# Which engine adds the block sums of the down and gate weights, and when the gate's first chunks are split

## The chip, the cores and the metric

The kernel runs on one core of a Trainium2 chip. The metric is the device time of one execution in microseconds (us); shorter is better. The engines are named as the profile names them: PE (matrix products, with PEld for its weight loads), DVE (vector), ACT (scalar), POOL (GpSimd) and SP (which here only issues DMAs).

## The reference

One layer of a decoder trunk over 512 tokens of width 1024, in fp32, and a final RMSNorm. The part that the change touches is the end of it:

```
h = rmsnorm(x, ffn_norm[i])
x = x + conv_ffn(h, w_up[i], conv_w[i], conv_b[i], w_down[i])
gate = sigmoid(rmsnorm(x, ple_norm[i]) @ w_ple_gate[i])
x = x + gate * (p[i] @ w_ple[i])
return rmsnorm(x, final_norm)
```

`conv_ffn` multiplies by `w_up` (1024 x 5632), runs a causal convolution of width 3, gates one half by the GELU of the other, and multiplies by `w_down` (2816 x 1024). The gate's weights are 1024 x 1024.

## The kernel before, in words

**Each fp32 product is three.** Every operand is cut into a rounded high part and the rest. For weights `parts` (L64 to 72) does it: ACT casts (`whi`, L69), DVE subtracts (`wlo`, L70). `mm3` (L203 to 207) then issues three matmuls, at L205, L206 and L207. A pair of cut tiles holds 1024 columns, and four pairs are in rotation (`WB = 4`); with `spare` the pair comes from the pool of 37 general 4 KB buffers (`blk`) instead.

**Seven products for eight.** The large square products follow a scheme in which a 2 x 2 block product takes seven block products, P1 to P7. Their weights are four blocks a, b, c, d and sums of them: P1 takes a, P2 takes d, P3 takes c, P5 takes t = b + a, P7 takes s = b + c, P6 takes t + c, P4 takes that + d. Each of them is handled in chunks of two 128-row slices (1024 columns); a product of n = 4 slices has two chunks, c0 and c1. `plan_seven` (L93 to 148) makes for each product and chunk a unit of two functions: `load` brings the blocks in, `cut` makes the high and low part. What computes the sums is its argument `adds`:

- "vector": blocks are loaded as they are, and all sums are DVE additions (L138) in `cut`.
- "some": t = b + a and s = b + c are made by the DMA: `get` loads b on SP's queue and adds the second block with an accumulating DMA on POOL's queue (`add_to`, L106). The additions of c for P6 and of d for P4 are DVE's, at L138.
- "all": as "some", but c and d are added to t by accumulating DMAs too, issued when P5 and P6 have been cut.

**The order.** `todo` is the list of units in the order of their use. `prepare` and `take` (L150 to 160) keep four loaded and two cut ahead of PE (four in the tail). All engines, and SP's and POOL's DMA queues, work in the order of the program, so an instruction that waits holds up all behind it. `seven` (L349 to 407) runs the products in a given order. Where P6 ends, its result is copied from PSUM to SBUF by ACT (`u`, L372), since P7 goes on in the same banks; PE's first matmul of P7 waits for that copy.

**The stages around the change.** The up projection is a loop of 22 steps (L689 to 717), two `proj8` of 24 matmuls each. The down projection is done in three parts, (0,4), (4,4) and (8,3), inside that loop after steps 8, 16 and 21, in the order DOWN = P1, P5, P2, P6, P7, P4, P3, all with "all". Parts 1 and 2 have two full chunks, part 3 a full and a half one. Its results are added to x by DVE (`drain_x`, L682). Then the tail: `turn_half` transposes x (PE L724, scaled by ACT, L727), `embed` multiplies by `w_ple` (L652), the loop that fills `XE` makes the seven operands of the gate (L746 to 757), and the gate's product runs in the order LAST = P5, P1, P6, P7, P4, P2, P3 with "some", as the last large product. Four small operations on POOL (L615) make the norms' factors between part 3 and the gate. After it come the sigmoid, the last sums and the output.

Of the kernel before, what the change touches and what calls it, by code (L numbers as in the profile page):

```python
# [20 lines left out]
KF = FF // P  # L21
# [12 lines left out]
INNER = ("P1", "P5", "P6", "P7", "P4", "P2", "P3")  # L34
DOWN = ("P1", "P5", "P2", "P6", "P7", "P4", "P3")
LAST = ("P5", "P1", "P6", "P7", "P4", "P2", "P3")
# [9 lines left out]
def trunk(ctx, tc, xT, xr, pT, wsT, par, bsp, w_u0, w_u1, w_v, w_ga, w_gb, w_p, w_pl,  # L46
# [28 lines left out]
    todo = []  # L75
# [9 lines left out]
    def pairs_of(n):  # L85

        return [(q, min(2, n - q)) for q in range(0, n, 2)]
# [5 lines left out]
    def plan_seven(w, order=INNER, adds="vector", spare=(), q0=0, n=HK):  # L93

        raw = {}

        def block_of(name, ch):  # L100
            q, m = ch
            return w("abdc".index(name), q0 + q, m)

        def fetch(t, name, ch, **kw):
            o = t[:, :ch[1] * T].rearrange("p (q f) -> p q f", q=ch[1])
            (G if kw else nc.sync).dma_start(o, block_of(name, ch), **kw)  # L106

        def add_to(t, name, ch):
            fetch(t, name, ch, accum_op=ALU.add)

        def get(name, ch, *blocks):
            if (name, ch) not in raw:
                t = raw[name, ch] = block("raw", (CW,))
                fetch(t, blocks[0], ch)
                for z in blocks[1:]:
                    add_to(t, z, ch)
            return raw[name, ch]

        def unit(prod, ch):
            inplace = adds == "vector"  # L120
            t = "a" if inplace else "t"
            need = {"P1": [("a", "a")], "P5": [("b", "b")] if inplace else [("t", "b", "a")],
                    "P6": [] if adds == "all" else [("c", "c")], "P7": [] if inplace else [("s", "b", "c")],
                    "P4": [] if adds == "all" else [("d", "d")], "P2": [("d", "d")], "P3": [("c", "c")]}[prod]
            dst = {"P1": "a", "P5": t, "P6": t, "P7": "b" if inplace else "s", "P4": t, "P2": "d", "P3": "c"}[prod]
            extra = {"P5": "b" if inplace else None, "P6": "c", "P7": "c" if inplace else None, "P4": "d"}.get(prod)
            if adds == "all":
                extra = None
            cols = ch[1] * T

            def load():
                for args in need:
                    get(args[0], ch, *args[1:])

            def cut():
                z = raw[dst, ch]
                if extra:
                    V.tensor_tensor(z[:, :cols], z[:, :cols], raw[extra, ch][:, :cols], op=ALU.add)  # L138
                o = parts(z, cols, spare=prod in spare)
                if adds == "all" and prod in ("P5", "P6"):  # L140
                    add_to(z, "c" if prod == "P5" else "d", ch)
                return o

            todo.append((load, cut))

        for prod in order:
            for ch in pairs_of(n):
                unit(prod, ch)

    def prepare(loads=LOADS):  # L150
        while todo and len(loaded) < loads:
# [5 lines left out]
    def take(ahead=AHEAD, loads=LOADS):  # L157
        while (todo or loaded) and len(ready) <= ahead:
            prepare(loads)
        return ready.pop(0)  # L160
# [7 lines left out]
    def blocks(w):  # L168

        return lambda b, q, m: w[b, q:q + m].rearrange("q p f -> p q f")  # L170

    for w in (w_v, w_ga, w_gb):
        plan_seven(blocks(w))

    def plan_map(g2):
        plan(w_pl[g2].rearrange("p g k d -> p (g k d)"))
# [14 lines left out]
    for i in range(KF):  # L191
        plan(w_up[2 * i].rearrange(flat))
        plan(w_up[2 * i + 1].rearrange(flat))

        part = done_at.get(i // 2) if i % 2 == 0 else done_at.get(KF // 2) if i == KF - 1 else None
        blocks_of_down.append(part)
        if part:
            plan_seven(blocks(w_dn), DOWN, "all", q0=part[0], n=part[1])
    for k in range(2):
        plan(w_ple[k])  # L200
    plan_seven(blocks(w_g), LAST, "some", spare=("P3",))

    def mm3(o, w, a, first, last, **kw):  # L203
        (wh, wl), (ah, al) = w, a
# [141 lines left out]
    ops = {"P1": ("a", "A11"), "P5": ("c", "D"), "P6": ("b", "S2"), "P7": ("b", "S3"), "P4": ("b", "A22"),  # L346
           "P2": ("a", "A12"), "P3": ("c", "E")}

    def seven(op, drain, order=INNER, fill=(), tail=False):  # L349

        fill = list(fill)
        n = len(op)
        ahead = AHEAD + 2 if tail else AHEAD
        bank_of = {}
        begun = set()
        u = [[None, None], [None, None]]

        def step(o, c, w, ch, first):  # L360
            for j, c0, m, t in o:
                for i in range(ch[1]):
                    k = ch[0] + i
                    a = op[k][c]
                    a = [a[:, z, j * P:(j + 1) * P] for z in range(2)]
                    mm3(t, a, [z[:, c0:c0 + m] for z in wslice(w, i, T)], first and k == 0, k == n - 1,
                        skip_group_check=True)

        def copies(i):
            for j in range(2):  # L370
                u[i][j] = work("u")
                S.copy(u[i][j], seeded[j])  # L372

        def minus(p, z):
            j, c0, m, t = p
            o = z[j][:, c0:c0 + m]
            V.tensor_tensor(o, t, o, op=ALU.subtract)
            return o

        for prod in order:  # L380
            b, c = ops[prod]
            if b not in bank_of:
                bank_of[b] = [(j, 0, T, seeded[j] if b == "b" else bank()) for j in range(2 if b != "c" or not tail else 1)]
                if b == "c" and tail:
                    bank_of[b] += [(1, 0, H, bank()[:, :H]), (1, H, H, bank()[:, :H])]
            o = bank_of[b]
            first = b != "b" and b not in begun
            begun.add(b)
            if prod == "P3" and tail:
                ws = [take(ahead) for _ in pairs_of(n)]  # L390
                for p in o:
                    for w, ch in zip(ws, pairs_of(n)):
                        step([p], c, w, ch, False)
                    drain(0, p[0], 1, minus(p, u[0]), p[1])
                continue
            for ch in pairs_of(n):
                step(o, c, take(ahead), ch, first)
                if fill:
                    fill.pop(0)()
            if prod == "P1":  # L400
                for j in range(2):
                    S.copy(seeded[j], o[j][3])
            elif prod == "P6":
                copies(0)
            elif prod == "P7":
                copies(1)
                for p in bank_of["c"]:
                    minus(p, u[1])
                for j in range(2):
                    drain(1, j, 1, u[1][j], 0)  # L410
            elif prod == "P4":
                for j in range(2):
                    drain(1, j, 0, seeded[j], 0)
            elif prod == "P2":
                for p in o:
                    drain(0, p[0], 0, p[3], 0)
            elif prod == "P3":
                for p in o:
                    drain(0, p[0], 1, minus(p, u[0]), 0)
        for f in fill:  # L420
            f()
# [17 lines left out]
    def load(k):  # L439
        if k % 2 == 0:  # L440
            x2.append(block("x"))
        x.append(x2[-1][:, k % 2])
        nc.sync.dma_start(x[k], xT[k])
# [3 lines left out]
    for k in range(KD):  # L447
# [3 lines left out]
        c = take(1, 1)  # L451
# [234 lines left out]

    hc = []
    first = None
    for i in range(KF):  # L689
        if i:  # L690
            o1, o2 = proj8(xg), proj8(xg)
        else:

            o1, o2 = bank(), bank()
            c = [take(), take()]
            for k in range(KD):
                for o, w in zip((o1, o2), c):
                    mm3(o, wslice(w, k), act(xg[k]), k == 0, k == KD - 1)
        a = conv(2 * i, o1)
        S.activation(a, a, AF.Gelu)  # L700
        b = conv(2 * i + 1, o2)
        V.tensor_tensor(a, a, b, op=ALU.mult)
        if i % 2 == 0:
            q = i // 2
            if q % 2 == 0 or any(q == q0 for q0, _ in PARTS):
                t11 = block("a11", (2, 2, H), F32R)
                n11 = 0
            cut_into(t11[:, n11], a[:, :H])
            first = a
        else:  # L710
            z = split(a)
            hc.append(dict(A11=t11[:, n11], A12=z[:, :, :H], A22=z[:, :, H:], **combine(first, a)))
            n11 += 1
        part = blocks_of_down[i]
        if part:
            q0, n = part
            seven(hc[q0:q0 + n], drain_x(q0 + n == KF // 2), DOWN)
# [28 lines left out]
    XE = []  # L746
# [41 lines left out]
                    V.tensor_scalar_mul(ot, ot, r)  # L788
                nc.sync.dma_start(out[b, :, g * T:(g + 1) * T], ot)

    seven(XE, drain_g, LAST, tail=True)


_ORDER = ["xT", "xr", "pT", "wsT", "par", "bsp", "w_u0", "w_u1", "w_v", "w_ga", "w_gb", "w_p", "w_pl",
# [72 lines left out]
```

## Time and profile before

| | |
|---|---|
| median of 3 runs | 807.81 us (807.12 to 807.92) |
| the profiled execution | 809.77 us, its span 808.1 us |
| PE busy | 773.3 us, 96% of the span |
| DVE, ACT, POOL busy | 553.9, 389.6, 60.5 us |
| mean granted clock of PE | 0.986 |

Times of the trace count from the start of the span; the profiled execution is 1.67 us longer than its span. "Idle before" is the time in which an engine had nothing to do ahead of an instruction, with the instruction that released it behind the arrow. A row of PE gives the start and the length of a matmul; they overlap, so that their pace is read from start to start.

### The profile page before, as it was taken

To read this page: it belongs to the slowest core of one execution; us is meant where nothing else is said; L and a number is where in the kernel's file an instruction comes from. 1 tells how busy PE (TensorE), PEld (TensorE's weight loads), DVE (VectorE), ACT (ScalarE), POOL (GpSimd) and SP (SyncE) were. 2 spreads that over 40 slices of the span, in tenths; PEclk is the share of its full clock that TensorE was granted. 3 is DMA by queue.
4 is the path that set the end of the run, shared out by engine and by line. 5 is a ranking of instruction groups with operands and counts; after the bars stand their busy time and mean duration, and the time that the engine had idled before them with its cause. 6 is when DMAs were issued, how large, how long until landed. Compare 5 with 4: busy or idle time off the path is not lost.

```text
span 808.1 us, 9316 instructions
## 1 busy us (share of the span) xinstructions
PE 773.3 (96%) x3458; PEld 635.6 (79%) x3458; DVE 553.9 (69%) x783; ACT 389.6 (48%) x566; POOL 60.5 (7%) x95
## 2 busy tenths in 40 slices
PE   9999999999999999999999997999999799999793
PEld 7888888888888887888888875888888588877673
DVE  7796988774666646336766663676774566778896
ACT  6676745562232324225644543345443434467873
POOL 0000100000122000000000021000013010031101
PEclk9999999999999999999999998999999899999997
DMA  9612225152044256006422369631229862391712
GB/s 350 253 53 79 78 79 183 53 191 96 1 156 150 85 173 218 1 1 268 174 53 66 91 133 269 216 93 46 78 79 212 244 168 78 107 194 26 239 22 104
DMA packets 42493, 104.26 MB, mean 129 GB/s; under 512 B 3664, under 2 KB 3792, under 8 KB 42448
## 3 DMA queue, kind: packets, MB, share of 16 engines
q1 hardware_dynamic: 33760, 85.73, 30.3%
q0 software_dynamic: 7104, 13.63, 10.0%
q10 hardware_dynamic: 1584, 4.31, 1.6%
q8 instruction: 27, 0.44, 0.2%
q14 instruction: 18, 0.15, 0.1%
HBM read 100.51 MB, written 3.15 MB: 128 GB/s over the span
## 4 chain that ended last, share of the span: by engine, by line
PE 47%; issue 27%; DMA 11%; DVE 8%; ACT 5%; POOL 1%; POOLq 0%; SPq 0%; ACTq 0%; DVEq 0%
PE mm L205 10%; PE mm L206 10%; PE mm L207 10%; DMA raw<-in_w_dn 9%; PE sd L205 6%; PE sd L206 6%; PE sd L207 6%; DVE wlo L70 2%; ACT whi L69 2%; DMA pt<-in_pT 1%; DVE raw L138 1%; POOL raw L106 1%; PE mm L514 1%; DVE x L773 0%; DVE ple L784 0%
## 5 line engine op out<-in xcount | busy, mean ns | idle before, releaser
L70 DVE TENSOR_TENSOR wlo<-raw,whi 128x1024 fp32r<-128x1024 f32 (+1 forms) x192 | 225.3, 1182 | 184.2 <-ACT whi L69 183.6
L69 ACT CAST whi<-raw 128x1024 fp32r<-128x1024 f32 (+1 forms) x185 | 189.8, 1032 | 232.4 <-PE mm L206 56.2
L206 PE MATMUL mm<-blk,whi 128*128 128x512 f32 x480 | 186.8, 389 | 0.0
L205 PE MATMUL mm<-blk,whi 128*128 128x512 f32 x480 | 186.4, 390 | 0.3 <-ACT blk L240 0.3
L207 PE MATMUL mm<-blk,wlo 128*128 128x512 f32 x480 | 186.6, 389 | 0.0
L205 PEld LDWEIGHTS mm<-blk,whi 128*128 128x128 f32 x480 | 90.0, 188 | 19.6 <-ACT blk L240 0.9
L206 PEld LDWEIGHTS mm<-blk,whi 128*128 128x128 f32 x480 | 90.1, 188 | 18.8
L207 PEld LDWEIGHTS mm<-blk,wlo 128*128 128x128 f32 x480 | 90.1, 188 | 18.6
L205 PE MATMUL mm<-whi,blk 128*128 128x512 f32 x214 | 83.9, 392 | 1.2 <-ACT xf L727 1.2
L206 PE MATMUL mm<-wlo,blk 128*128 128x512 f32 x214 | 83.4, 390 | 0.0
L207 PE MATMUL mm<-whi,blk 128*128 128x512 f32 x214 | 83.3, 389 | 0.0
L205 PE MATMUL sd<-whi,cmb 128*128 128x512 f32 x108 | 45.5, 421 | 12.8 <-ACT u L372 12.3
L205 PE MATMUL mm<-whi,cmb 128*128 128x512 f32 (+1 forms) x132 | 50.1, 380 | 2.1 <-ACT xf L727 1.8
L106 POOL DMA_DIRECT2D raw<-in_w_dn x24 | 27.9, 1389 | 321.9 <-DVE wlo L70 207.6
L206 PE MATMUL mm<-wlo,cmb 128*128 128x512 f32 (+1 forms) x132 | 49.8, 377 | 0.4 <-DVE wlo L70 0.4
L207 PE MATMUL mm<-whi,cmb 128*128 128x512 f32 (+1 forms) x132 | 49.3, 376 | 0.0
L205 PEld LDWEIGHTS mm<-whi,blk 128*128 128x128 f32 x214 | 40.2, 188 | 10.3 <-ACT xf L727 2.0
L207 PEld LDWEIGHTS mm<-whi,blk 128*128 128x128 f32 x214 | 40.2, 188 | 8.3
L206 PEld LDWEIGHTS mm<-wlo,blk 128*128 128x128 f32 x214 | 40.2, 188 | 8.2
L206 PE MATMUL sd<-wlo,cmb 128*128 128x512 f32 x108 | 44.3, 410 | 0.3 <-DVE wlo L70 0.3
L207 PE MATMUL sd<-whi,cmb 128*128 128x512 f32 x108 | 43.9, 408 | 0.0
L205 PE MATMUL sd<-whi,blk 128*128 128x512 f32 x110 | 43.1, 392 | 0.5 <-ACT u L372 0.5
(184 smaller groups left out, 1037.2 us busy)
## 6 DMA issues: line engine op xcount, KB each, us to landing
raw<-in_w_up SPq DMA_DIRECT2D x44, 512.0 KB, 5.5
raw<-in_w_dn SPq DMA_DIRECT2D x25, 512.0 KB, 3.4
raw<-in_w_dn POOLq DMA_DIRECT2D x20, 512.0 KB, 7.8
raw<-in_w_g SPq DMA_DIRECT2D x10, 512.0 KB, 6.7
raw<-in_w_v SPq DMA_DIRECT2D x8, 512.0 KB, 11.4
raw<-in_w_ga SPq DMA_DIRECT2D x8, 512.0 KB, 4.0
raw<-in_w_gb SPq DMA_DIRECT2D x8, 512.0 KB, 3.6
raw<-in_w_p SPq DMA_DIRECT2D x8, 512.0 KB, 4.8
```

Source lines behind the costliest of these rows:

```text
L69: (V.tensor_copy if first else S.copy)(hi[:, :cols], raw[:, :cols])
L70: V.tensor_tensor(lo[:, :cols], raw[:, :cols], hi[:, :cols].bitcast(F32), op=ALU.subtract)
L106: (G if kw else nc.sync).dma_start(o, block_of(name, ch), **kw)
L138: V.tensor_tensor(z[:, :cols], z[:, :cols], raw[extra, ch][:, :cols], op=ALU.add)
L205: PE.matmul(o, wh, ah, start=first, stop=False, **kw)
L206: PE.matmul(o, wh, al, start=False, stop=False, **kw)
L207: PE.matmul(o, wl, ah, start=False, stop=last, **kw)
L514: PE.matmul(mx[:, n * P:(n + 1) * P], vt[n].rearrange("p a t -> p (a t)")[:, f * P:(f + 1) * P], wsm[:, f, :], start=True, stop=True)
```

## The change

The down weights change from "all" to "some". The gate's weights change from "some" to "all", with the cut tiles of P5, P1 and P3 in the general buffers. The gate's first four units (P5 c0, P5 c1, P1 c0, P1 c1) leave the list: they are loaded at the end of steps 17 to 20 of the up loop and cut at the end of steps 18 to 21, and `seven` takes them from a list.

```diff
@@ plan_seven
-            todo.append((load, cut))
-
-        for prod in order:
-            for ch in pairs_of(n):
-                unit(prod, ch)
+            return load, cut
+
+        return [unit(prod, ch) for prod in order for ch in pairs_of(n)]
@@
     for w in (w_v, w_ga, w_gb):
-        plan_seven(blocks(w))
+        todo.extend(plan_seven(blocks(w)))
@@
         if part:
-            plan_seven(blocks(w_dn), DOWN, "all", q0=part[0], n=part[1])
+            todo.extend(plan_seven(blocks(w_dn), DOWN, "some", q0=part[0], n=part[1]))
     for k in range(2):
         plan(w_ple[k])
-    plan_seven(blocks(w_g), LAST, "some", spare=("P3",))
+
+    gate_units = plan_seven(blocks(w_g), LAST, "all", spare=("P5", "P1", "P3"))
+    early = gate_units[:4]
+    todo += gate_units[4:]
@@ seven
-    def seven(op, drain, order=INNER, fill=(), tail=False):
+    def seven(op, drain, order=INNER, fill=(), tail=False, given=()):
...
+        given = list(given)
...
-                step(o, c, take(ahead), ch, first)
+                step(o, c, given.pop(0) if given else take(ahead), ch, first)
@@ up loop
+    split_early = []
     for i in range(KF):
...
+        for j, (load, cut) in enumerate(early):
+            if i == KF - 5 + j:
+                load()
+            if i == KF - 4 + j:
+                split_early.append(cut())
         part = blocks_of_down[i]
@@ tail
-    seven(XE, drain_g, LAST, tail=True)
+    seven(XE, drain_g, LAST, tail=True, given=split_early)
```

**First place: POOL's queue at part 1 of the down projection.** The tiles in rotation are t of c0 (`raw_3629`), t of c1 (`raw_3686`), s of c0 and s of c1; `raw_4553` and `raw_4610` are t of part 2. Before:

```order
L106 DMA raw_3629<-in_w_dn 128x2x512 x2
L106 DMA raw_3686<-in_w_dn 128x2x512 x2
L106 DMA raw_3819<-in_w_dn 128x2x512
L106 DMA raw_3838<-in_w_dn 128x2x512
L106 DMA raw_3629<-in_w_dn 128x2x512
L106 DMA raw_3686<-in_w_dn 128x2x512
L106 DMA raw_4553<-in_w_dn 128x2x512 x2
```

The second transfer to a t tile adds c and waits until that tile has been cut for P5; the third adds d and waits for the cut for P6. Now:

```order
L106 DMA raw_3629<-in_w_dn 128x2x512
L106 DMA raw_3686<-in_w_dn 128x2x512
L106 DMA raw_3821<-in_w_dn 128x2x512
L106 DMA raw_3840<-in_w_dn 128x2x512
L106 DMA raw_4553<-in_w_dn 128x2x512
```

Four transfers are left of eight, and none of them waits for a cut; part 2 has the same rows with its own tiles.

**Second place: DVE in part 3, around the start of P6.** `raw_5259` and `raw_5310` are t of the full and of the half chunk, `x_2521` and `x_2522` take the result of P2. In the change:

```order
L70 TENSOR_TENSOR wlo_5459<-raw_5403,whi_5458 128x512
L138 TENSOR_TENSOR raw_5259<-raw_5259,raw_5421 128x1024
L138 TENSOR_TENSOR raw_5310<-raw_5310,raw_5437 128x512
L684 TENSOR_TENSOR x_2521<-mm_5401,x_2521 128x512
L70 TENSOR_TENSOR wlo_5473<-raw_5259,whi_5472 128x1024
L70 TENSOR_TENSOR wlo_5490<-raw_5310,whi_5489 128x512
L684 TENSOR_TENSOR x_2522<-mm_5402,x_2522 128x512
L138 TENSOR_TENSOR raw_5259<-raw_5259,raw_5342 128x1024
L138 TENSOR_TENSOR raw_5310<-raw_5310,raw_5403 128x512
```

Before, the same stretch had no L138, and both low parts of P6 stood ahead of the x sums:

```order
L70 TENSOR_TENSOR wlo_5410<-raw_5318,whi_5409 128x1024
L333 TENSOR_TENSOR cmb_5370<-e_5362,cmb_5370 128x2x256
L70 TENSOR_TENSOR wlo_5429<-raw_5375,whi_5428 128x512
L70 TENSOR_TENSOR wlo_5442<-raw_5241,whi_5441 128x1024
L70 TENSOR_TENSOR wlo_5459<-raw_5286,whi_5458 128x512
L682 TENSOR_TENSOR x_2521<-mm_5373,x_2521 128x512
L682 TENSOR_TENSOR x_2522<-mm_5374,x_2522 128x512
```

So the x sum that needs the end of P2 has moved ahead of the two low parts that P6's second matmul needs.

**Third place: POOL's queue from the early gate units to the gate's product.** `in_w_g` are the gate's weights, `fr` the factors of the norms. In the change the four rows of `in_w_g` at the top are t of c0 (+ a, + c) and t of c1 (+ a, + c), the three further down s of c0 and d for both t, the last one s of c1:

```order
L106 DMA raw<-in_w_g 128x2x512 x4
L106 DMA raw<-in_w_dn 128x2x512
L106 DMA raw<-in_w_dn 128x512
L106 DMA raw<-in_w_dn 128x2x512
L106 DMA raw<-in_w_dn 128x512
L106 DMA raw<-in_w_g 128x2x512 x3
L617 TENSOR_TENSOR fr<-fms,neghalf 128x1 x4
L106 DMA raw<-in_w_g 128x2x512
L617 TENSOR_TENSOR fr<-fms,neghalf 128x1 x4
```

Before, from within part 3 on, with t of both chunks ahead of the factors and s of both behind them:

```order
L106 DMA raw<-in_w_dn 128x2x512
L106 DMA raw<-in_w_dn 128x512
L106 DMA raw<-in_w_dn 128x2x512
L106 DMA raw<-in_w_dn 128x512
L106 DMA raw<-in_w_g 128x2x512 x2
L615 TENSOR_TENSOR fr<-fms,neghalf 128x1 x4
L106 DMA raw<-in_w_g 128x2x512 x2
L615 TENSOR_TENSOR fr<-fms,neghalf 128x1 x4
```

The gate's t are now loaded ahead of part 3's own sums (the four rows of `in_w_dn`), and of the two s, which both stood behind the first four factors, c1 alone still does.

## Rows read from the trace of the kernel before

**Rows 1.** The page: PE's busy time, and the chain that ended last, by engine.

```profile
PE 773.3 (96%) x3458; PEld 635.6 (79%) x3458; DVE 553.9 (69%) x783; ACT 389.6 (48%) x566; POOL 60.5 (7%) x95
PE 47%; issue 27%; DMA 11%; DVE 8%; ACT 5%; POOL 1%; POOLq 0%; SPq 0%; ACTq 0%; DVEq 0%
```

**Rows 2.** Busy time by stretch: gate products, part 2, up steps (columns: first line).

```profile
core 0: us, PE busy (x) PEld busy (x) DVE busy (x) ACT busy (x) POOL busy (x), PEclk, DMA share, GB/s
200.00:300.00 100.00, 100.00 (x443) 82.84 (x442) 61.43 (x90) 28.34 (x33) 12.28 (x18) 1.00 0.30 107
...
620.00:640.00 20.00, 14.60 (x54) 11.53 (x53) 7.33 (x7) 6.76 (x8) 1.62 (x2) 0.83 1.02 267
...
660.00:700.00 40.00, 40.00 (x178) 33.12 (x177) 29.52 (x43) 17.74 (x26) 0.00 (x0) 1.00 0.29 85
```

**Rows 3.** PE in order of time, parts 1 and 2: start, length, what, [idle before].

```profile
472.73 0.39 PE L205 MATMUL mm<-whi,a 128*128 128x512 f32 x1
...
500.39 0.79 PE L205 MATMUL sd<-whi,cmb 128*128 128x512 f32 x1 [5.07 <-ACT u L372]
...
506.10 0.43 PE L206 MATMUL sd<-wlo,cmb 128*128 128x512 f32 x1
...
519.56 0.39 PE L205 MATMUL mm<-blk,whi 128*128 128x512 f32 x1
...
606.60 0.39 PE L205 MATMUL mm<-whi,a 128*128 128x512 f32 x1
...
633.92 0.80 PE L205 MATMUL sd<-whi,cmb 128*128 128x512 f32 x1 [5.40 <-ACT u L372]
...
652.87 0.39 PE L205 MATMUL mm<-blk,whi 128*128 128x512 f32 x1
```

**Rows 4.** The chain that ended last, in parts 1 and 2: start, length, what.

```profile
486.21 12.49 DMA raw<-in_w_dn
498.81 1.04 ACT whi L69
...
614.89 17.35 DMA raw<-in_w_dn x2
```

**Rows 5.** Line 106: ns on POOL (least, median, most), POOL's waits, time to landing.

```profile
L106 POOL DMA_DIRECT2D raw<-in_w_dn x24: 894/1198/2193, 408.7 to 718.0; - x24
...
L106 POOL DMA_DIRECT2D raw<-in_w_g x4: 1195/1623/2567, 718.6 to 763.2; - x4
...
  DVE wlo L70: 222.2, 12
...
DMA to landing us min/median/max: 2.5/4.8/13.4
```

**Rows 6.** Line 138, the sums on DVE: ns of one (least, median, most).

```profile
L138 DVE TENSOR_TENSOR raw<-raw x28: 1217/1222/1518, 48.6 to 771.4; 128x1024 f32<-128x1024 f32 x28
```

**Rows 7.** DMA issues between 644 and 660 us: queue, count, size, us to landing.

```profile
raw<-in_w_dn POOLq DMA_DIRECT2D x1, 512.0 KB, 5.7
```

**Rows 8.** PE in order of time: the first matmul of part 3, the first transpose behind it.

```profile
707.27 0.39 PE L205 MATMUL mm<-whi,a 128*128 128x512 f32 x1
...
738.31 0.93 PE L724 MATMUL mm<-ident,x 128*128 128x128 f32 x7
```

**Rows 9.** POOL in order of time, in the tail.

```profile
745.85 1.57 POOL L615 TENSOR_TENSOR fr<-fms,neghalf 128x1 f32<-128x1 f32 x2 [0.33 <-DVE fms L613]
761.96 2.47 POOL L106 DMA_DIRECT2D raw<-in_w_g  x2 [14.55 <-DVE wlo L70]
```

**Rows 10.** The chain that ended last, in the tail.

```profile
753.13 1.14 DVE raw L138
...
757.75 1.14 DVE wlo L70
```

**Rows 11.** PE in order of time: the first matmul of the gate's P6, the last matmul.

```profile
766.46 0.50 PE L205 MATMUL sd<-whi,s 128*128 128x512 f32 x1 [0.43 <-ACT sd L402]
...
795.57 0.28 PE L207 MATMUL mm<-whi,cmb 128*128 128x256 f32 x1
```

## The prediction

> **What bounds the kernel now.** I read the page first: PE is busy for 96% of the span, and still only 47% of the chain that ended last is PE; DMA holds 11% of it [rows 1]. So PE's queue sets the time, and the few us in which it stands still are what a change can win. Next the busy time by stretch, to find them: PE is at 100% in the products in the middle and in the up steps, and at 14.60 of 20 us in the middle of part 2, with the granted clock at 0.83 and the DMA share at 1.02 [rows 2]. Then PE in order of time shows what stood there: ahead of the first matmul of P7 it is idle for 5.07 us in part 1 and for 5.40 us in part 2, both released by ACT's copy u [rows 3]. That copy was not slow but late: the chain has ahead of it a DMA of the down weights and one cast, 12.49 us and 1.04 us in part 1, and two DMAs in a row, 17.35 us, in part 2 [rows 4]. These are accumulating transfers on POOL. With "all", c goes to t after the cut for P5, and d after the cut for P6; POOL stands 222.2 us over the run in 12 waits for such cuts [rows 5], and the s for P7 queue behind them. The cast that needs the last transfer (d, for P4) stands ahead of the copy u on ACT, and P7 waits for the copy.
>
> After each stall PE runs at half its pace for a while: from 500.39 to 506.10 us there are 13 matmuls, 0.44 us each. Those are the lower one of its two clock levels (1.2 against 2.4 GHz). The 59 left of that part take 13.46 us, 0.228 each [rows 3].
>
> **Parts 1 and 2.** Seven products of two chunks are 168 matmuls, 38.3 us at 0.228. Part 1 takes 46.83 us from its first matmul to the next up matmul, part 2 takes 46.27 [rows 3]. The excess, 8.5 and 8.0 us, is stall, half pace and a few tenths. The change takes four of eight accumulating transfers out of each part, and those that remain wait for no cut. What moves to DVE is four sums of 1.22 us per part [rows 6]; they need plain loads that are issued ahead, and the order has all four ahead of the x sums of P2. So no cast on ACT in front of the copy u waits for a transfer issued late. Do the sums fit? The middle products use "vector", with four such sums per chunk against two now, and DVE is 61% busy there while PE stays at 100% [rows 2]; in part 2's stretch it is busy for 7.33 of 20 us, so that 4.9 us more in 38 are covered by idle time. If the cover were gone, part of 4.9 us per part would show. I take the whole excess: **8.5 + 8.0 = 16.5 us**, bounds 12 (a third stays, as other small gaps or half pace) and 16.5.
>
> **Early gate units.** Four casts (1.04 us, [rows 4]) and four subtractions (about a sum's 1.22 us) come into the up steps 18 to 21, one pair each. DVE is busy for 29.52 of 40 us there and ACT for 17.74 [rows 2]; a step takes 48 matmuls, 10.9 us, so DVE goes from 8.0 to 9.3 us of it. That fits; cost 0. The loads lie in a stretch with a DMA share of 0.29. The cast of t of c1 waits for its transfer + a, which stands on POOL behind the + c of c0, and that behind the cut of c0 one step earlier: two issues at 1.2 us [rows 5] and a landing of 5.7 us in a quiet stretch [rows 7] are 8.1 us, against a step of 10.9. PE has two cut pairs (10.9 us of matmuls) in hand behind it; cost 0, bounds 0 and 3.
>
> **Part 3.** It has 126 matmuls, 28.7 us, and takes 31.04 [rows 8]: an excess of 2.3 us. The stalls that go are small here. New is that the x sum which needs the end of P2 stands on DVE ahead of P6's low parts: half a sum of 1.22 us and a subtraction of 1.14 [rows 6, 10], of which some 0.7 us pass before P2's last bank is done, so P6 waits about 1 us at its second matmul. P7 and P4 lose a few tenths in the same way. A new excess of 2.3 in place of the old one: **gain 0**. The loads of the last blocks wait for buffers that the last up matmuls free, and so start around the part's start. s for P7 must be loaded, and then added to. Two issues and a landing of 8.7 us (half of the 17.35, [rows 4]) end some 11 us after the start; ACT reaches that cast at about 13 to 16 us, behind P1, P5 and P2 (54 matmuls, 12.3 us). Bounds: +1.4 (all gaps but P6's close) and -3 (late by a landing's spread).
>
> **Tail.** The loop before the gate's product loses one cast on ACT and, on DVE, one sum and one subtraction that the chain holds: 1.14 + 1.14 us [rows 10]. But the s of c1 is issued only behind the four factors, at 745.85 + 1.57 = 747.4 us [rows 9], and lands 5.7 to 8.7 us later, at 753.1 to 756.1, while ACT wants it at about 753.6 with the casts of the loop behind it. I take half of the 2.3 us: 1.2. From P6 of the gate to the last matmul there are five products, the columns of 120 matmuls, 27.4 us; they take 29.1 [rows 11], since the s came at 761.96 us [rows 9] and P6's split beside it. P6 is now split during part 3's end, so I take 1.5 of the 1.7. **Sum 2.7**, bounds 0.5 and 4.0. The output after the last matmul is untouched.
>
> **A rule that speaks against it.** POOL's issues of line 106 have taken from 894 to 2567 ns beside a working DVE [rows 5], and DVE's sums at most 1518 against 1222 ns [rows 6]: neither is held for long. The Trainium skill (SBUF — State Buffer, section "Who interferes with whom") says that a DVE instruction with two SBUF inputs contends with GpSimd instructions that read SBUF, and that a DMA issued from GpSimd can starve when its descriptors cannot be written; it infers that tensor-tensor operations spare the writing. By it more sums on DVE could delay the sums left on POOL; the rows agree with the milder reading.
>
> **Sum.** 16.5 + 0 + 0 + 2.7 = 19.2 us. The profiled execution took 809.77 us, which gives 790.6; it lies 1.96 us (0.24%) above the median, and I put the difference on the median: 807.81 - 19.2 = **788.6 us**. All lower bounds together are 12 - 3 - 3 + 0.5 = 6.5 us (801), all upper ones 16.5 + 1.4 + 4.0 = 21.9 (785.9).
>
> **Rivals.**
> 1. *The stall moves to part 3 and the tail* (0.18). Loads, gate transfers and the two s of part 3 crowd at its start; a pair of sums that takes the 17.35 us of [rows 4] ends some 20 us after the start in place of 11, so P7 there is late by about 4 us, with 2.8 us of half pace (13 times 0.44 - 0.228) behind it; the s of c1 in the tail adds up to 2 us. 19.2 - 4 - 2.8 - 1.2 = 11.2: 796.6 us. For it: the share of 1.02 in part 2. Against it: parts 1 and 2 no longer load the queues alike, and the gate's t are out of the way before part 3.
> 2. *One of parts 1 and 2 keeps its stall*, because a plain load of c or d waits for a buffer that is now held longer (0.05): 8 us less, 796.6 us as well. Against it: those loads are issued well ahead of the stretch.
> 3. *POOL is slowed by DVE's sums* (0.04): each issue at the longest row, 2567 in place of 1198 ns, is 1.4 us more; it counts once for the two s of part 3 (2.8 us, of which some 1.5 are slack) and once in the tail: 19.2 - 1.3 - 1.4 = 16.5, 791.3 us. It is the Trainium skill's rule above (SBUF — State Buffer), taken hard.
> 4. *Slower* (0.03): the early casts block ACT. If the cast of the gate's t of c1, and then that of part 3's t, waits for POOL, the convolution's reads of PSUM and the next up casts stand behind it. PE has 10.9 us in hand; beyond that each us is lost, with 2.8 us of half pace. To undo 19.2 us and add 1.6, two such waits must last 10.9 + 20.8/2 - 2.8 = 18.5 us each. The longest landing of line 106 was 13.4 us [rows 5], so it takes a queue behind a queue: with 20 us each, 811 us.
> 5. *No change* (0.02): two of these at once, or a cause behind the stall other than POOL's order; about 807.
>
> **How the numbers follow.** 0.68 is left for the forecast, in its own bounds of about 786 to 794. 0.2% (1.6 us) is what a measurement here can tell from no change. Faster by more: the forecast, rivals 1 to 3, 0.94 with a little taken off for rival 1 at its worst; the same 0.03; slower 0.03. The range goes from 785.5, just past the sum of the upper bounds, to 797, which takes in rivals 1 to 3 as priced; beyond it lie 4, 5 and a worse 1.
>
> **What would show it.** Right: no idle over 1 us before `sd` matmuls in parts 1 and 2, the clock at 1.00 there, each part at 38 to 39 us; POOL's wait for `wlo` far under 222.2 us; 12 transfers of `in_w_dn` on POOL, and 28 - 4 + 12 = 36 sums at line 138; a gap of about 1 us at P6 of part 3. Wrong: an idle of several us before P7 in part 3 with ACT's cast released by a DMA (rival 1), in part 1 or 2 (rival 2), issues on POOL above 2 us throughout (rival 3), gaps in the up steps after 660 us (rival 4). The step most likely off is the tail's 2.7.

## The result, and the profile after

The changed kernel takes **793.3 us** (median of 4 runs, 792.52 to 794.14), the kernel before 807.87 us (median of 4). The ratio is 0.9818, with a 95% interval of 0.9801 to 0.9836. That is 14.6 us faster, inside the range that was given (785.5 to 797.0), and 4.7 us short of the forecast of 788.6. The profiled execution took 794.14 us, its span 792.4 us.

The kernel after has one line more ahead of `mm3`, so that its matmuls are L206, L207 and L208; ACT's copy u is L374, the scaled transposes are L735, the transposes themselves L732, the x sums L684. The page after, PE's busy time and the chain by engine, as in [rows 1]:

```profile
PE 768.7 (97%) x3458; PEld 634.4 (80%) x3458; DVE 561.7 (71%) x791; ACT 389.4 (49%) x566; POOL 51.6 (7%) x87
PE 86%; DVE 7%; ACT 2%; DMA 2%; issue 1%; POOL 1%; POOLq 0%; SPq 0%; ACTq 0%; DVEq 0%
```

The chain that ended last is now PE's for 86% of the span, where it was 47%, and the DMAs hold 2% of it, where they held 11%. PE in order of time after (start, length, what, [idle before]), the rows that answer to [rows 3, 8, 11]:

```profile
471.93 0.39 PE L206 MATMUL mm<-whi,a 128*128 128x512 f32 x1
...
510.01 0.39 PE L206 MATMUL mm<-blk,whi 128*128 128x512 f32 x1
...
597.05 0.39 PE L206 MATMUL mm<-whi,a 128*128 128x512 f32 x1
...
635.13 0.39 PE L206 MATMUL mm<-blk,whi 128*128 128x512 f32 x1
...
689.53 0.39 PE L206 MATMUL mm<-whi,a 128*128 128x512 f32 x1
...
703.66 0.50 PE L207 MATMUL sd<-wlo,cmb 128*128 128x512 f32 x1 [1.01 <-DVE wlo L70]
...
720.57 1.91 PE L732 MATMUL mm<-ident,x 128*128 128x128 f32 x16
...
743.73 0.80 PE L206 MATMUL mm<-whi,cmb 128*128 128x512 f32 x1 [4.54 <-ACT xf L735]
...
752.19 0.39 PE L206 MATMUL sd<-whi,s 128*128 128x512 f32 x1
...
779.87 0.28 PE L208 MATMUL mm<-whi,cmb 128*128 128x256 f32 x1
```

No row with an idle time is left in parts 1 and 2. The differences of these starts, beside those of before, account for the whole span ("loop" is from the first transpose behind part 3 to the first matmul of the gate's P6):

| stretch | before, us | after, us | forecast gain | measured gain |
|---|---|---|---|---|
| up to part 1 | 472.73 | 471.93 | 0 | 0.80 |
| part 1 | 46.83 | 38.08 | 8.5 | 8.75 |
| up steps between | 87.04 | 87.04 | 0 | 0 |
| part 2 | 46.27 | 38.08 | 8.0 | 8.19 |
| up steps with the early cuts | 54.40 | 54.40 | 0 | 0 |
| part 3 | 31.04 | 31.04 | 0 | 0 |
| loop | 28.15 | 31.62 | 1.2 | -3.47 |
| gate's P6 to the last matmul | 29.11 | 27.68 | 1.5 | 1.43 |
| after the last matmul | 12.53 | 12.53 | 0 | 0 |
| sum | 808.1 | 792.4 | 19.2 | 15.7 |

The first line is not the change's: in the kernels below, whose code is the same up to there, part 1 starts between 471.38 and 473.83 us. All that is missing is in the loop. There the trace after shows one stall of 4.54 us, and 14 matmuls from 743.73 to 749.87 us at 0.44 us each behind it, at a granted clock of 0.50 (columns as in [rows 2]):

```profile
743.73:749.87 6.14, 6.14 (x14) 4.79 (x15) 5.84 (x14) 3.73 (x8) 0.00 (x0) 0.50 0.93 330
```

It has the same pattern as the stalls that went from parts 1 and 2. What ACT waited for, and what POOL did before that (three views of after, each in order of time: ACT, POOL, the chain):

```profile
735.45 0.83 ACT L735 ACTIVATE xf<-mm,pr 128x256 f32<-128x256 f32 x2
740.56 1.04 ACT L69 CAST whi<-raw 128x1024 fp32r<-128x1024 f32 x1 [4.29 <-DMA raw<-in_w_g]
```

```profile
724.97 1.20 POOL L106 DMA_DIRECT2D raw<-in_w_g  x1 [24.18 <-DVE wlo L70]
726.74 1.19 POOL L106 DMA_DIRECT2D raw<-in_w_g  x1 [0.57 <-issue]
727.49 1.82 POOL L617 TENSOR_TENSOR fr<-fms,neghalf 128x1 f32<-128x1 f32 x2
729.64 1.56 POOL L617 TENSOR_TENSOR fr<-fms,neghalf 128x1 f32<-128x1 f32 x2 [0.33 <-DVE fms L615]
731.17 1.20 POOL L106 DMA_DIRECT2D raw<-in_w_g  x1
```

```profile
731.17 9.37 DMA raw<-in_w_g
```

The last POOL row is the s of the gate's second chunk. It is issued behind two transfers that wait for P6's cuts (+ d) and behind the four factors, 10.6 us after part 3's end, and takes 9.37 us to land. ACT is free for its cast at 736.28 us and stands until 740.56, with the casts of the loop behind it.

Line 106 after (ns on POOL: least, median, most; POOL's waits), as in [rows 5]:

```profile
L106 POOL DMA_DIRECT2D raw<-in_w_dn x12: 1185/1198/1887, 408.0 to 695.0; - x12
...
L106 POOL DMA_DIRECT2D raw<-in_w_g x8: 1185/1197/1687, 625.2 to 731.2; - x8
...
  DVE wlo L70: 76.8, 4
```

Twelve transfers for the down weights, eight for the gate, and POOL's wait for cuts down from 222.2 to 76.8 us.

### The profile page after: what moved, and what is told of

The parts are those of the page before. It is cut to its first block, busy times and chain, and to the rows that moved or that the text cites. A ratio compares the mean times of both kernels' runs of the same rounds, so it can differ in the third digit from the quotient of the medians.

```text
span 792.4 us, 9303 instructions
## 1 busy us (share of the span) xinstructions
PE 768.7 (97%) x3458; PEld 634.4 (80%) x3458; DVE 561.7 (71%) x791; ACT 389.4 (49%) x566; POOL 51.6 (7%) x87
## 4 chain that ended last, share of the span: by engine, by line
PE 86%; DVE 7%; ACT 2%; DMA 2%; issue 1%; POOL 1%; POOLq 0%; SPq 0%; ACTq 0%; DVEq 0%
PE mm L206 22%; PE mm L207 22%; PE mm L208 22%; PE sd L206 6%; PE sd L207 6%; PE sd L208 6%; DVE wlo L70 2%; DMA raw<-in_w_g 1%; ACT whi L69 1%; DVE raw L138 1%; POOL fr L617 1%; PE mm L516 1%; PE mm L632 0%; DMA x<-in_xT 0%; DVE x L781 0%
## 5 line engine op out<-in xcount | busy, mean ns | idle before, releaser
L206 PE MATMUL mm<-blk,whi 128*128 128x512 f32 x480 | 186.4, 390 | 0.5 <-ACT blk L241 0.5
L207 PE MATMUL mm<-blk,whi 128*128 128x512 f32 x480 | 186.8, 389 | 0.0
L208 PE MATMUL mm<-blk,wlo 128*128 128x512 f32 x480 | 186.6, 389 | 0.0
L206 PEld LDWEIGHTS mm<-blk,whi 128*128 128x128 f32 x480 | 90.0, 188 | 19.9 <-ACT blk L241 0.8
L207 PEld LDWEIGHTS mm<-blk,whi 128*128 128x128 f32 x480 | 90.1, 188 | 18.7
L208 PEld LDWEIGHTS mm<-blk,wlo 128*128 128x128 f32 x480 | 90.1, 188 | 18.7
L206 PE MATMUL mm<-whi,blk 128*128 128x512 f32 x214 | 83.7, 392 | 1.2 <-ACT xf L735 1.2
L207 PE MATMUL mm<-wlo,blk 128*128 128x512 f32 x214 | 83.4, 390 | 0.0
L208 PE MATMUL mm<-whi,blk 128*128 128x512 f32 x214 | 83.3, 389 | 0.0
L206 PE MATMUL mm<-whi,cmb 128*128 128x512 f32 (+1 forms) x132 | 51.0, 387 | 4.5 <-ACT xf L735 4.5
L207 PE MATMUL mm<-wlo,cmb 128*128 128x512 f32 (+1 forms) x132 | 50.8, 385 | 0.0
L208 PE MATMUL mm<-whi,cmb 128*128 128x512 f32 (+1 forms) x132 | 50.8, 384 | 0.0
L206 PEld LDWEIGHTS mm<-whi,blk 128*128 128x128 f32 x214 | 40.2, 188 | 10.3 <-ACT xf L735 2.0
L208 PEld LDWEIGHTS mm<-whi,blk 128*128 128x128 f32 x214 | 40.2, 188 | 8.4
L207 PEld LDWEIGHTS mm<-wlo,blk 128*128 128x128 f32 x214 | 40.2, 188 | 8.1
L206 PE MATMUL sd<-whi,cmb 128*128 128x512 f32 x108 | 42.6, 397 | 0.8 <-ACT u L374 0.8
L206 PE MATMUL sd<-whi,blk 128*128 128x512 f32 x110 | 43.1, 392 | 0.3 <-ACT u L374 0.3
L207 PE MATMUL sd<-wlo,cmb 128*128 128x512 f32 x108 | 42.3, 392 | 1.1 <-DVE wlo L70 1.0
L207 PE MATMUL sd<-wlo,blk 128*128 128x512 f32 x110 | 42.8, 389 | 0.0
L208 PE MATMUL sd<-whi,blk 128*128 128x512 f32 x110 | 42.8, 389 | 0.0
## 6 DMA issues: line engine op xcount, KB each, us to landing
raw<-in_w_v SPq DMA_DIRECT2D x8, 512.0 KB, 11.3
```

Of the source, the lines that this page charges most:

```text
L206: PE.matmul(o, wh, ah, start=first, stop=False, **kw)
L207: PE.matmul(o, wh, al, start=False, stop=False, **kw)
L208: PE.matmul(o, wl, ah, start=False, stop=last, **kw)
```

## The experiments

Each was run beside the kernel before; ratios are to it. Parts and stretches are read from PE's starts as in the table above, each from one traced execution. That execution lies within 1.5 us of its run's median, save for `gate_only` (815.16 us, 4.1 above) and `d_on_dve` (799.34 us, 3.2 above), whose stretches may be long by as much in all.

**Which half of the change brings the gain?** `down_only` is the kernel before with one word changed:

```diff
-            plan_seven(blocks(w_dn), DOWN, "all", q0=part[0], n=part[1])
+            plan_seven(blocks(w_dn), DOWN, "some", q0=part[0], n=part[1])
```

> The kernel before with the down weights on "some" and the gate left as it was. Theory (the gain is all in parts 1 and 2 of the down projection, where no sum waits for a cut any more, and the gate's part of the change cost time): parts 1 and 2 take 38.1 us each, part 3 about 31, the tail as before; 807.9 - 16.9 = 791 us, a little faster than the whole change at 793.3. Rival (the gate's sums crowd part 3 unless they are made early): part 3 or the tail grows by 5 us or more, 796 us or above.

Measured: 790.98 us, ratio 0.9793 (0.9777 to 0.9809). Parts 1 and 2 take 38.08 us each, part 3 30.58, the loop 28.94, P6 to the end 29.10. The total is the theory's. The one word alone beats the whole change by 2.3 us (its slowest run took 792.40 us, the fastest of the change 792.52).

`gate_only` is the changed kernel with the down weights left on "all":

```diff
-            todo.extend(plan_seven(blocks(w_dn), DOWN, "some", q0=part[0], n=part[1]))
+            todo.extend(plan_seven(blocks(w_dn), DOWN, "all", q0=part[0], n=part[1]))
```

> The change with the down weights left on "all". Theory: the stalls ahead of P7 in parts 1 and 2 stay at 5 us and more (46 to 47 us each), and the loop before the gate's product loses what it lost in the change; 807.9 + 2 = 810 us. Rival (the early gate units are what frees the queues): under 804 us.

Measured: 811.05 us, ratio 1.0042 (1.0027 to 1.0057). PE in order of time, the rows with more than 2 us of idle from part 1 on:

```profile
500.39 0.79 PE L206 MATMUL sd<-whi,cmb 128*128 128x512 f32 x1 [5.15 <-ACT u L374]
...
634.52 0.79 PE L206 MATMUL sd<-whi,cmb 128*128 128x512 f32 x1 [5.51 <-ACT u L374]
...
728.01 0.78 PE L206 MATMUL sd<-whi,cmb 128*128 128x512 f32 x1 [2.20 <-ACT u L374]
...
766.01 0.80 PE L206 MATMUL mm<-whi,cmb 128*128 128x512 f32 x1 [4.80 <-ACT xf L735]
```

The two old stalls stand where they were [rows 3], part 3 has grown to 34.94 us with a third, and the last row is the loop's new stall. So the gain is the down weights' alone, and the loss comes with the gate. The longer part 3 was not expected; which of the gate's early units lengthens it was not tried.

**What is the stall in the loop?** `s_early` is the changed kernel with this ahead of the tail, which loads two units more, so that s of the gate's c1 stands on POOL ahead of both + d and of the factors:

```diff
+    while todo and len(loaded) < 6:
+        load, cut = todo.pop(0)
+        load()
+        loaded.append(cut)
     G1 = []
```

> The change, with two more units loaded ahead of the tail, so that the sum s of the gate's second chunk is issued on POOL ahead of the four factors instead of behind them. Theory (the cast of that s waits since its transfer is issued too late): the 4.5 us stall before the last matmuls of P5 and P1 and the half pace behind it go, 793.3 - 6 = 787 us, 786 to 789. Rival (the transfer is slow because the reloaded embeddings, the last norm's weights and the gate's last blocks are in flight with it, whenever it is issued): ACT still waits 2 us or more for it, 790 to 793 us.

Measured: 788.68 us, ratio 0.9761 (0.9743 to 0.9779). The loop takes 25.83 us in place of 31.62. POOL and PE in order of time:

```profile
705.41 1.20 POOL L106 DMA_DIRECT2D raw<-in_w_g  x1 [4.33 <-DMA raw<-in_w_g]
724.73 1.19 POOL L106 DMA_DIRECT2D raw<-in_w_g  x1 [18.12 <-DVE wlo L70]
```

```profile
739.93 0.50 PE L206 MATMUL mm<-whi,cmb 128*128 128x512 f32 x1 [0.95 <-ACT xf L735]
```

The second s goes out at 705.41 us, and the idle at that matmul falls from 4.54 to 0.95 us, with no half pace behind it. So the stall is this transfer's, and an early issue removes it. The rival is wrong in its "whenever it is issued", but the landing was slow at the late place: issues and their times to landing, in the loop of the change (730.5 to 742 us), and then in `s_early` (704 to 712 us):

```profile
ple<-ple_d SPq DMA_DIRECT2D x4, 256.0 KB, 7.1
gB<-in_gfin ACTq DMA_DIRECT2D x1, 512.0 KB, 5.7
raw<-in_w_g POOLq DMA_DIRECT2D x1, 512.0 KB, 9.4
```

```profile
raw<-in_w_g POOLq DMA_DIRECT2D x1, 512.0 KB, 5.6
```

With the change's issue at 731.17 us and the 5.6 us of the quieter stretch, s would have landed at 736.8, about 0.5 us after ACT was free; that is an estimate from these rows. By it the stall took both, the late issue and the slow landing. That the loads beside it (the embeddings `ple`, the last norm's weights `gB`) are what slows it was not tried.

**Is the gate's half worth anything?** `no_early` is the changed kernel with no unit cut early:

```diff
-    early = gate_units[:4]
-    todo += gate_units[4:]
+    early = gate_units[:0]
+    todo += gate_units[0:]
```

> The change without the early loads and cuts: the gate's first four units come from the list as all others. Theory (with "all" the sums for P6 wait for the cuts of P5, which now lie in the tail): P6's cast waits for + c and blocks ACT before the product; a stall of 5 to 10 us with half pace behind it, 797 to 804 us. Rival (the early cuts buy nothing, since two units were cut ahead anyway): 792 to 794 us.

Measured: 804.74 us, ratio 0.9963 (0.9951 to 0.9975), just above the theory's range. The loop takes 38.76 us, P6 to the end 33.30. PE waits twice for work that ACT does late. The chain has the transfer + c of c0 ahead of the first wait (PE in order of time; the chain), and one of the late s, 13.15 us from 747.77 us, ahead of the second:

```profile
750.36 1.22 PE L206 MATMUL mm<-whi,cmb 128*128 128x512 f32 x2 [8.31 <-ACT whi L69]
...
762.52 0.79 PE L206 MATMUL sd<-whi,s 128*128 128x512 f32 x1 [2.69 <-ACT sd L404]
```

```profile
732.22 7.85 DMA raw<-in_w_g
```

"All" for the gate without early cuts is what "all" was for the down weights: each sum waits for a cut.

`down_s10` puts the early s on `down_only`, with the gate as it was before:

```diff
+    while todo and len(loaded) < 10:
+        load, cut = todo.pop(0)
+        load()
+        loaded.append(cut)
     G1 = []
```

> The down weights on "some", and the gate as it was before ("some", nothing cut early), but with all units up to the gate's P7 loaded ahead of the tail, so that both s are issued ahead of the four factors. It asks whether the gate's part of the change is worth anything once s is early. Theory (the 1.4 us that the change won from P6 to the end come from s and P6's cut being there in time, and the loop before keeps one cast, one sum and one subtraction more): from P6 to the end 27.7 us in place of 29.1, the loop at 27.5 to 29, 788.5 to 790.5 us, so that the gate's part is worth 0.5 to 2 us. Rival (the early cuts are worth more): 791 us or more. Other rival (they are worth nothing): 788 us or less.

Measured: 796.17 us, ratio 0.9856 (0.9831 to 0.9881). P6 to the end is 27.64 us, as the theory said, but the loop is 32.65. The casts and subtractions in the loop, by line (count, busy us, mean ns; idle before), of `down_s10`:

```profile
L69 ACT CAST whi<-raw 128x1024 fp32r<-128x1024 f32 x8 | 8.3, 1045 | 4.0 <-PE mm L207 4.0
L70 DVE TENSOR_TENSOR wlo<-raw,whi 128x1024 fp32r<-128x1024 f32 x8 | 9.8, 1220 | 1.7 <-ACT whi L69 1.6
```

and of `s_early`:

```profile
L69 ACT CAST whi<-raw 128x1024 fp32r<-128x1024 f32 x3 | 3.2, 1059 | 0.3 <-PE mm L208 0.3
L70 DVE TENSOR_TENSOR wlo<-raw,whi 128x1024 fp32r<-128x1024 f32 x5 | 6.1, 1223 | 1.0 <-ACT whi L69 1.0
```

Eight casts against three, eight subtractions against five, and three sums besides. PE stands for 8.8 us in that loop, each time until ACT is done, and for 3.7 us in the loop of `s_early`. This fell on the first rival's side: with s early on both, the gate's part (early cuts, and its sums by DMA) is worth 796.2 - 788.7 = 7.5 us. That early cuts take this work out of the loop into the up steps is the likely cause; the two pieces were not run apart. The expectation took `down_only`'s loop of 28.94 us for granted; it has four casts and five subtractions there, since its last cuts wait for s. So s early, without the gate's part, cost 796.2 - 791.0 = 5.2 us, and against `down_only`, the fastest kernel run without the gate's part, that part with s early is worth 791.0 - 788.7 = 2.3 us.

**Which transfer made the stalls of parts 1 and 2?** `c_on_dve` is the kernel before with c for P6 added on DVE and d still by transfer; `d_on_dve` the other way round. With "c", `cut` of P6 adds c on DVE and then issues + d; with "d", `cut` of P5 issues + c, and `cut` of P4 adds d on DVE. One line of the edit (the lists of plain loads and of sums on DVE follow it):

```diff
-                if adds == "all" and prod in ("P5", "P6"):
+                if prod in {"all": ("P5", "P6"), "c": ("P6",), "d": ("P5",)}.get(adds, ()):
                     add_to(z, "c" if prod == "P5" else "d", ch)
```

> The kernel before, with only the addition of c (for P6) of the down weights moved to DVE; d is still added to t by a transfer on POOL behind the cut for P6. Theory A (the transfers + c wait first and hold back the sums s and + d behind them, so that all land in one crowd): without them s and + d go out early enough, parts 1 and 2 take 38 to 40 us each, 791 to 795 us. Theory B (the trouble is that the cast of t + d stands ahead of the copy u on ACT and waits for a transfer that has to follow the cut for P6): the stall ahead of P7 stays at 4 us or more, 45 us a part, 803 us or more.

> The kernel before, with only the addition of d (for P4) moved to DVE; c is still added to t by a transfer behind the cut for P5. Theory A: + c still holds back the two s; the casts for P6 and P7 wait, 40 to 43 us a part, 797 to 803 us. Theory B: nothing ahead of the copy u waits for a late transfer, the stalls go whole, 38 to 39 us a part, 790 to 793 us.

Measured: `c_on_dve` 800.6 us, ratio 0.9906 (0.9881 to 0.9931), parts 39.88 and 43.48 us; `d_on_dve` 796.16 us, ratio 0.9845 (0.9822 to 0.9867), parts 40.04 and 44.34. Neither theory holds: each of the two sums, left as a transfer, keeps most of part 2's stall of 5.40 us and about a third of part 1's 5.07 (1.47 and 1.65 us). PE in part 2, `c_on_dve` first:

```profile
625.57 0.56 PE L205 MATMUL sd<-whi,cmb 128*128 128x512 f32 x1 [3.50 <-ACT u L372]
```

```profile
625.80 0.50 PE L205 MATMUL sd<-whi,cmb 128*128 128x512 f32 x1 [4.06 <-ACT u L372]
```

POOL and the chain of `c_on_dve` there:

```profile
612.42 3.65 POOL L106 DMA_DIRECT2D raw<-in_w_dn  x3 [20.90 <-DVE wlo L70]
```

```profile
613.14 9.80 DMA raw<-in_w_dn
...
624.00 1.04 ACT whi L69
```

And the chain of `d_on_dve`; in both, the copy u follows this cast:

```profile
609.74 13.43 DMA raw<-in_w_dn
...
624.23 1.04 ACT whi L69
```

In both, three transfers go out in one burst when a cut is done. Among them is the s of P7's second chunk (second of the three in `c_on_dve`, behind + d of c0; third in `d_on_dve`, behind + c of c1). It waits for no cut itself, and lands 9.80 and 13.43 us after its issue. This suggests that what matters is a transfer waiting for a cut ahead of s, whichever it is.

`all_s_first` tests that without moving a sum: the kernel before, "all" throughout, with s loaded together with t:

```diff
-            need = {"P1": [("a", "a")], "P5": [("b", "b")] if inplace else [("t", "b", "a")],
+            need = {"P1": [("a", "a")], "P5": [("b", "b")] if inplace else [("t", "b", "a")] + ([("s", "b", "c")] if adds == "all" else []),
```

> The kernel before (all sums of the down weights by DMA, as many transfers as before), but with the two s for P7 loaded together with the t for P5, so that they stand on POOL ahead of most transfers that wait for a cut. Theory (the stall ahead of P7 comes from the order: s stands behind a transfer that waits for a cut, and lands 10 us after it): the stalls shrink to 0 to 2 us, parts 1 and 2 take 38 to 42 us each, 792 to 799 us. Rival (there are simply too many accumulating transfers for the time, in whatever order): 45 us a part and more, 805 us or more.

Measured: 802.02 us, ratio 0.9922 (0.9901 to 0.9943), parts 42.09 and 43.11 us. The stall ahead of P7 has gone in part 1 and is 0.45 us in part 2, with as many transfers as before; but there is a new one of 2.03 us ahead of P4, in both. PE in order of time (part 1), and the chain there:

```profile
501.65 0.58 PE L205 MATMUL sd<-whi,blk 128*128 128x512 f32 x1 [2.03 <-ACT u L372]
```

```profile
480.61 7.02 DMA raw<-in_w_dn
...
487.73 1.06 ACT whi L69
...
488.81 1.24 DVE wlo L70
...
490.34 8.70 DMA raw<-in_w_dn
```

So the order of s made the stall at P7. It did so partly through another transfer: in the kernel before, the last to land ahead of the copy u is + d of c0, 12.49 us after its issue at 486.21 [rows 4]; with s out of that burst the same transfer, issued at 484.95, lands in 7.24 us. Behind this stands a second limit: + c, the cut for P6, + d, one after the other for the tile of the second chunk, 18.4 us from 480.61 to 499.04. The forecast of this run missed that; the total came out 3 us above its range. Moving the sums to DVE removes both at once.

**Is DVE's part really free?** `double_sum` repeats one subtraction of the same size for each P6 and P4 chunk of the down weights in the changed kernel:

```diff
                 o = parts(z, cols, spare=prod in spare)
+                if adds == "some" and prod in ("P6", "P4"):
+                    V.tensor_tensor(o[1][:, :cols], z[:, :cols], o[0][:, :cols].bitcast(F32), op=ALU.subtract)
```

> The change, with one operation of a sum's size (the subtraction for the low part, done a second time) added on DVE for each P6 and P4 chunk of the down weights: as much DVE work again as the change moved there, 4.9 us in each of parts 1 and 2 and about 3.7 in part 3. Theory (DVE has room in parts 1 and 2, and none around the start of P6 in part 3): parts 1 and 2 stay at 38.1 us, part 3 grows by 1 to 3 us, 794 to 797 us. Rival (DVE is near its limit there too): 38.1 grows by over 1 us a part, 798 us or more.

Measured: 796.56 us, ratio 0.9857 (0.9835 to 0.9878). Parts 1 and 2 stay at 38.08 us; part 3 grows from 31.04 to 34.65. Busy time by stretch, part 1 first of `double_sum` and then of the change (columns as in [rows 2]):

```profile
471.40:509.50 38.10, 38.10 (x170) 31.55 (x169) 33.30 (x35) 18.80 (x23) 0.00 (x0) 1.00 0.61 206
```

```profile
471.90:510.00 38.10, 38.10 (x169) 31.54 (x168) 29.10 (x31) 19.07 (x23) 0.00 (x0) 1.00 0.66 209
```

DVE at 33.30 of 38.1 us still costs nothing in parts 1 and 2. In part 3 it has no room: PE's idle at P6's second matmul grows from 1.01 to 2.75 us, and the part by 3.6 us, a little more than the 1 to 3 expected.

**Can part 3 be had cheaper?** `best_s1` is `s_early` with the early units one up step earlier:

```diff
-            if i == KF - 5 + j:
+            if i == KF - 6 + j:
                 load()
-            if i == KF - 4 + j:
+            if i == KF - 5 + j:
```

> The change with the early sum s of the run before (788.7 us), and the gate's four early units loaded and cut one up step earlier, so that the last of their subtractions is out of DVE's queue at the start of part 3. Theory (DVE works without a break from the start of part 3 to P6, but P6's low part also stands behind an x sum that waits for PE): part 3 shrinks by 0 to 0.8 us, 787.9 to 788.7 us. Rival (the subtraction was what made P6 late): part 3 shrinks by 1.2 us or more, 787.5 or less.

Measured: **788.05 us**, ratio 0.9749 (0.973 to 0.9767), the fastest median of all, though the 0.6 us to `s_early` is within the spread of the runs. Part 3 takes 30.56 us in place of 31.05. Its idle at P6 falls from 1.01 to 0.79 us: the x sum ahead of the low part still waits for PE.

`best_d3s1` has, on top of that, only d on DVE in part 3, and c by transfer (`plan_seven` is edited as for `d_on_dve`):

```diff
-            todo.extend(plan_seven(blocks(w_dn), DOWN, "some", q0=part[0], n=part[1]))
+            todo.extend(plan_seven(blocks(w_dn), DOWN, "some" if part[0] < 8 else "d", q0=part[0], n=part[1]))
```

> The fastest version so far (788.05 us: the change, the gate's s early, its early units one step earlier), with only part 3 changed: there c is added to t by DMA again and d stays on DVE. Theory (in part 3 P6's low part is late because the sum of c comes late in DVE's full queue, and c's transfer has time since P5's cut lies in the up loop): part 3 falls from 30.6 to about 29.5 us, 787 us. Rival (the transfer lands late in the crowd of loads at the part's start): part 3 at 31 us or more, 788.5 us or more.

Measured: 793.38 us, ratio 0.9819 (0.9802 to 0.9836); part 3 takes 35.55 us. P6's idle is down to 0.25 us, as the theory had it, but P7 pays, and the total falls on the rival's side. POOL, the chain and PE:

```profile
690.12 4.37 POOL L106 DMA_DIRECT2D raw<-in_w_dn  x4 [7.48 <-DVE wlo L70]
```

```profile
692.14 15.24 DMA raw<-in_w_dn
```

```profile
710.80 0.50 PE L206 MATMUL sd<-whi,cmb 128*128 128x512 f32 x1 [3.95 <-ACT u L374]
```

Four transfers (+ c twice, then both s) go out in one burst behind the cuts for P5, among the loads at the part's start, and the first s lands after 15.24 us. This is the size that the prediction's first rival had for part 3, with another cause: there the two s alone were to be slow, here + c stands ahead of them.

## Why the prediction was right or wrong

- **Parts 1 and 2, 16.5 us: right** (16.94), and so was the cause. `down_only` shows that it is the down weights' step alone, `double_sum` that the DVE sums cost nothing there. On the mechanism the text was half explicit: it named s queueing behind the cuts and the cast of d's sum ahead of the copy u. The runs show that either of the two sums is enough to hold s back for part of the stall, and that + c, cut, + d is a chain of its own behind it (`all_s_first`). Of POOL's 222.2 us in 12 waits, 14.55 us are the gate's s [rows 9], which waits for no cut for P5 or P6; this changes nothing.
- **Early gate units, 0: right.** The up steps take 54.40 us before and after.
- **Part 3, 0: right**, both in the sum (31.04 us twice) and in its place: PE waits 1.01 us at P6's second matmul for the low part on DVE. The old gaps at P7 and P4 (1.07 and 0.49 us) went and new ones at P6 and P4 (1.01 and 0.26) came; that the sums agree to 0.01 us is chance. The bound for a late s did not come; `best_d3s1` shows how close it lay.
- **P6 to the end, 1.5: right** (1.43).
- **The loop, 1.2: wrong, it lost 3.47.** This is the whole miss, and the text had named the tail as the step most likely off. The step that failed is "the s of c1 is issued only behind the four factors, at 745.85 + 1.57 = 747.4 us [rows 9], and lands 5.7 to 8.7 us later, at 753.1 to 756.1, while ACT wants it at about 753.6 with the casts of the loop behind it. I take half of the 2.3 us: 1.2." The place was right, and two sizes were off to the same side. Counted from part 3's end, the text's issue is at 9.1 us, its landing at 14.8 to 17.8 and ACT's wish at 15.3. Measured were an issue at 10.6 (the two + d of the gate came in ahead of the factors) and a landing at 20.0 (9.37 us, above the range taken), with ACT ready at 15.7, close to the text. The price was wrong in kind too: the 2.8 us of half pace that rival 1 carried were not charged here, though the loop's gap was as open to it. The 2.3 us itself was right: with s early the loop takes 25.83 us, 2.32 less than before. The tail's lower bound, +0.5, was broken (it lost 2.04 us in all), and the rows allowed that: 8.7 us was half of two transfers' 17.35, but a single one has 12.49 [rows 4] and the longest 13.4 [rows 5]. In the trace of before, the gate's own two t, issued at 718.6 and 719.3 us, took 11.3 us (median):

```profile
raw<-in_w_g POOLq DMA_DIRECT2D x2, 512.0 KB, 11.3
```

- **Rivals.** Rival 1 came true in its tail half only, and larger than its 2 us there. Rivals 2 and 4 did not come: no stall in part 1 or 2, none in the up steps. Rival 3 did not either: the median issue on POOL is 1198 ns after as it was before, with eight sums more on DVE. The issue at 724.97 us, which had a subtraction beside it on DVE for nearly all its length, took 1.20 us like the others; beside the longest one before, 2567 ns, no sum or subtraction of weights ran; it stood close behind another issue. These rows agree with the milder reading of the Trainium skill's rule (SBUF — State Buffer, "Who interferes with whom"). Rival 4's sum is off by itself: two waits of 20 us at its prices lose 23.8 us, which gives 812.4 us and not 811; it did not come.

## What to carry to other kernels

A queue that works in order makes a transfer with a wait into a wait for everything behind it: before moving sums between a DMA queue and an engine, list what stands behind each wait, and where each landing is wanted. A transfer that waits for nothing belongs ahead of the ones that wait, and ahead of small operations on the same queue; that alone was worth 4.6 us in `s_early`. It is no gain by itself: in `down_s10` the same move cost 5.2 us, with casts and subtractions that then fell into the loop. When a cast's data come close to the time it is wanted, price the miss with everything that stands behind it, the half pace of PE included, and take the landing time from the longest rows of the busiest stretch; a burst's span divided by the number of its transfers is not a landing time.

## What was not expected of the hardware

The time from issue to landing of one 512 KB accumulating transfer spreads more than the prediction's 5.7 to 8.7 us: 5.6 us in `s_early`, 7.02 us and 8.70 us in the chain of `all_s_first`, 9.37 in the tail after, 9.80 and 13.43 as one of a burst of three, and 15.24 as one of four among loads. And half pace does not always begin where a stall ends: behind the 4.54 us in the loop after, 14 matmuls are slow from the first on, while behind `d_on_dve`'s 4.06 us in part 2 the first five start 0.22 to 0.34 us apart, and the slow ones, 0.43 us apart, come from 627.14 to 630.13 us, at a granted clock of 0.50. What decides that was not tried.
